# Sixteen of 22 feature tiles by seven products, and partial sums put into PSUM by ScalarE

## The chip, the cores and the metric

The kernel runs on one core of one Trainium2 chip. The metric is device time in microseconds of one execution: the median of 3 runs before the change is 2388.46 us (2387.38 to 2388.64). Engines are named as the profile names them: PE is TensorE (matmul), PEld its weight loads, DVE is VectorE, ACT is ScalarE, POOL is GpSimd, SP is SyncE, which issues the loads.

## The reference

Two layers; each is a feed-forward block, a mixing block of three kinds of attention, and a second feed-forward block, with a norm ahead of and behind each. The change touches the four feed-forward blocks alone. 512 tokens, model width 1024, feed-forward width 2816 = 22 tiles of 128 features.

```python
D_MODEL, SEQ, DEPTH = 1024, 512, 2
D_FF = ((8 * D_MODEL // 3 + 127) // 128) * 128        # 2816

def _swiglu(t, w_gate, w_up, w_down):
    return (jax.nn.silu(t @ w_gate) * (t @ w_up)) @ w_down

for l in range(DEPTH):
    f = _swiglu(_rmsnorm(h, ffn1_pre_g[l]), ffn1_w_gate[l], ffn1_w_up[l], ffn1_w_down[l])
    h = h + 0.5 * _rmsnorm(f, ffn1_post_g[l])
    ...                                               # mixing: three attentions, gates, output product
    f = _swiglu(_rmsnorm(h, ffn2_pre_g[l]), ffn2_w_gate[l], ffn2_w_up[l], ffn2_w_down[l])
    h = h + 0.5 * _rmsnorm(f, ffn2_post_g[l])
```

## The kernel before, in words

**Arithmetic.** Every factor is split into a high and a low part (`split`: ScalarE casts the high part, VectorE subtracts for the low part), and `mm3` makes one product of three matmuls of 128x512: high by high (L214), low by high (L215 or L216), high by low. The four feed-forward blocks are called a0, c0 (first layer) and a1, c1.

**Feature tiles in three ways.** Of the 22 feature tiles of a block, tiles 0 and 1 are "halved": they are made in two halves of the tokens, so that they can begin before the norm is done for all tokens (`halved`, L801 and L802). Plain pairs (14 and 15, 16 to 21) are made feature-major, with `gates` and `ups`, at full width. Twelve tiles (2 to 13) are made in three groups of four (`group`, `gate_up`): the input is cut into two halves of the tokens and of the width, the weights (two gate tiles and two up tiles side by side) likewise, and a 2x2 block product is made from seven block products in place of eight. `ORDER = (0, 2, 3, 4, 5, 1, 6)` is the order of the seven; `BlockUnit` makes their weights (one or two loads of 512 KB, up to two VectorE passes of 128x1024, a cast by ScalarE and a low part by VectorE), and `sums` with `whole`, `block_sum` and `parts_of` makes the sums of the input's blocks (L679, L685, L188, L189). The result of a group is token-major and is turned into feature-major by 16 transposes (`feature_major`, L761).

The seven products of a group write three pairs of PSUM banks: product 0 opens one that 3, 5 and 6 go on with; product 2 opens one that 4 goes on with; product 1 has its own. After a product, the banks are copied out by ScalarE or added to a tile `c..` in SBUF by VectorE (L744).

**Down.** The first 16 feature tiles go through `downs(0)` and `downs(1)`, again by seven block products (`product`, `first_factor`), the last six in `down` (plain), whose results VectorE adds to what lies in SBUF (`down_out`, L827; at the kernel's end `last_part`, L580). The seven products of `downs` are woven with the last plain pairs.

**What sets the order.** A queue `Q` holds jobs (weights to load, a generator that yields matmuls); loads are made ahead of their jobs as rings allow. Then a scheduler orders each engine's instructions within the dependences. PSUM has eight banks: four with the tag "mm" and four with the tag "z". Weight parts have rings of four (`wh`, `wl`).

Of the kernel before, what the change touches and what calls it, by code (L numbers as in the profile page):

```python
# [22 lines left out]
def kernel(  # L23
# [494 lines left out]
    class Sub:  # L518
# [57 lines left out]
        def last_part(self, t, hf, c, pt, i):  # L576

            f, h, st = self.fs[t], hT[t], self.sf[t]
            s, fc, w = tmp(f"fe{i}"), f[:, HF[hf]][:, c], slice(0, c.stop - c.start)
            nc.vector.tensor_tensor(s[:, w], fc, pt, ALU.add)  # L580
            self.squared(s[:, w], st, 2 * i, s[:, S // 2:])
            nc.vector.scalar_tensor_tensor(fc, s[:, w], RS * (0.5 if self.half else 1.0), self.gp[:, HF[hf]][:, c],
                                           ALU.mult, ALU.mult)
# [54 lines left out]
    TG = (2, 6, 10)  # L638

    HR = ("q", "q", "o", "o", "o", "tri", "tri", "rs")  # L640
    ORDER = (0, 2, 3, 4, 5, 1, 6)

    def ffn(l, src, wg, wu, wd, dst, name, spare, aside=None):
# [9 lines left out]
        def hidden(f, pg, pu):  # L653
            s = tmp(f"s{name}_{f}")
            nc.scalar.activation(s[:], pg[:], AF.Silu)
            if f < NC * FC:
                nc.vector.tensor_tensor(pair(f)[:, f % 2], pu[:], s[:], ALU.mult)
                return
            nc.vector.tensor_tensor(s[:], pu[:], s[:], ALU.mult)
            t = blk("q" if f >= 20 else "o", f"hid{name}_{f}")  # L660
# [61 lines left out]
        def gate_up(f, n, uns):  # L722
            if n in (0, 1, 2):
                st["gb", SUM[n]] = [pbank("mm", f"pt{name}_{f}_{n}_{e}") for e in range(2)]
            pts = st["gb", SUM[n]]
            opens, ends = n in (0, 1, 2), n in (1, 4, 6)
            for un in uns:
                for k in range(un.nk):
                    kk = un.k0 + k
                    for e in range(2):  # L730
                        mm3(pts[e][:], *input_block(n, kk, e), un.h[:, k], un.l[:, k], opens and kk == 0,
                            ends and kk == ND // 2 - 1, free=True)
                        yield 3 * S * PE_US
            i, j = TO[n]
            if n in (0, 2, 3, 6):
                st["c", i, j] = stile([P, 2, S], "f", f"c{name}_{f}_{i}{j}", F32)
            t = st["c", i, j]
            for e in range(2):
                if n == 6:
                    nc.scalar.activation(t[:, e], pts[e][:], AF.Silu)  # L740
                elif n in (0, 2, 3):
                    nc.scalar.copy(t[:, e], pts[e][:])
                else:
                    nc.vector.tensor_tensor(t[:, e], t[:, e], pts[e][:], ALU.add)  # L744
            if n == 1:
                nc.scalar.activation(t[:], t[:], AF.Silu)
            if n in (1, 6):
                u = st["c", i, 1]
                nc.vector.tensor_tensor(u[:], u[:], t[:], ALU.mult)
                st["hid", f, i] = u  # L750

        def feature_major(f):

            for i in range(2):
                u = st.pop(("hid", f, i))
                for b in range(2):
                    f2 = f + 2 * b
                    pt = pbank("z", f"th{name}_{f2}_{i}")
                    for m in range(2):
                        for e in range(2):  # L760
                            nc.tensor.transpose(pt[:, (2 * m + e) * P:(2 * m + e + 1) * P],  # L761
                                                u[:, e, (2 * b + m) * P:(2 * b + m + 1) * P], ident[:])
                    yield 0.45
                    out_ = pt[:].rearrange("p (m q) -> p m q", m=2)
                    nc.scalar.copy(pair(f2)[:, :, HALVES[i]], out_)

        def group(f):

            keep = Keep(lambda i, k0: stile([P, 2, S], "v", f"kt{name}_{f}_{i}_{k0}", F32)[:])
            for n in ORDER:  # L770
# [4 lines left out]
                yield uns, (lambda n=n, uns=uns: gate_up(f, n, uns))  # L775
            yield [], lambda: feature_major(f)
# [7 lines left out]
        def halved(f, ug, uu, half):  # L784
            if half == 0:
                st["p"] = [pbank("mm", f"p{x}{name}_{f + m}") for x in "gu" for m in range(2)]
            else:
                Q.hold, Q.pinned = False, True
                Q.load_ahead()
                Q.pinned = False  # L790
            c = HALVES[half]
# [29 lines left out]
        def down_out(t, hf, pt, last):  # L821
            f = dst.fs[t][:, HF[hf]]
            if not last:
                nc.vector.tensor_tensor(f, f, pt, ALU.add)
                return f
            s = tmp(f"f{name}_{t}")
            nc.vector.tensor_tensor(s[:], f, pt, ALU.add)  # L827
            return s[:]
# [28 lines left out]
        def product(ci, n, uns):  # L857
# [4 lines left out]
            if n in (0, 1, 2):  # L862
# [3 lines left out]
            opens, ends = n in (0, 1, 2), n in (1, 4, 6)  # L866
# [40 lines left out]
        def plain(f, *n):  # L907

            ug = wpair(wg[l], ND, f * P, f"g{name}_{f}")
            uu = wpair(wu[l], ND, f * P, f"u{name}_{f}")  # L910
            Q.add(ug, lambda: gates(f, ug))
            some(n[0])
            behind()
            Q.add(uu, lambda: ups(f, uu))
            some(n[1])

# [9 lines left out]
        ug, uu = wpair(wg[l], ND, 0, f"g{name}_0"), wpair(wu[l], ND, 0, f"u{name}_0")  # L926
# [3 lines left out]
        Q.add(ug + uu, lambda: halved(0, ug, uu, 0), src.ready((0, 1)))  # L930
        Q.add([], lambda: halved(0, ug, uu, 1), src.ready(range(NT)))
        Q.add([], lambda: iter(park() or ()))
        marks["first"] = len(Q.jobs)
        summed = sums()
        todo = iter([([], lambda: iter(next(summed) or ()))] * 3)
        plain(14, 1, 1)
# [3 lines left out]
        some(1)  # L940
        todo = turns(2)
        some(7)
        for g in (6, 10):
# [6 lines left out]
        todo = iter(())  # L950
        pairs = [(wpair(wg[l], ND, f * P, f"g{name}_{f}"), wpair(wu[l], ND, f * P, f"u{name}_{f}")) for f in (16, 18)]
        Q.add(pairs[0][0], lambda: gates(16, pairs[0][0]))
        behind()
        todo = downs(0)
# [8 lines left out]
        xg, xu = wpair(wg[l], ND, 20 * P, f"g{name}_20"), wpair(wu[l], ND, 20 * P, f"u{name}_20")  # L963
        Q.add(xg, lambda: gates(20, xg))
# [3 lines left out]
        Q.add(xu, lambda: ups(20, xu))  # L968
# [11 lines left out]
        down(wd[l, f0 * P:], NF - f0, hact, down_out, f"d{name}", dst, marks, reload)  # L980
        return marks

    def down(w, ktiles, act, emit, name, dst, marks, before=None):
# [7 lines left out]
        PAIRS = ((0, 1), (2, 3))  # L991

        def tiles(uns, hf, ts, done=None):
            pts = [pbank("mm", f"p{name}_{hf}_{t}") for t in ts]
            for un in uns:
                for k in range(un.nk):
                    kk = un.k0 + k
                    for t, pt in zip(ts, pts):
                        ah, al = act(kk, slice(t * P, (t + 1) * P))
                        mm3(pt[:], ah, al, un.h[:, k], un.l[:, k], kk == 0, kk == ktiles - 1)  # L1000
                        yield 3 * S * PE_US
                if done is not None:
                    done()
            last = len(ts) == 1
            for t, src in [(t, emit(t, hf, pt[:], last)) for t, pt in zip(ts, pts)]:
                dst.result(t, hf, src)

        def at_last(uns, hf, t):

            parts = [(c, pbank("mm", f"p{name}_{hf}_{t}_{i}")) for i, c in enumerate(HALVES)]  # L1010
            for i, (c, pt) in enumerate(parts):
                for un in uns:
                    for k in range(un.nk):
                        kk = un.k0 + k
                        ah, al = act(kk, slice(t * P, (t + 1) * P))
                        mm3(pt[:, c], ah, al, un.h[:, k, c], un.l[:, k, c], kk == 0, kk == ktiles - 1)
# [3 lines left out]
        def late(uns, hf, t):  # L1020
            if t == NT - 1 and dst.g_pre is None and hf == 0:
# [727 lines left out]
```

## Time and profile before

| | |
|---|---|
| median of 3 runs | 2388.46 us |
| span of the profiled execution | 2385.9 us |
| median less span | 2.6 us |
| granted clock | 1.000 |
| TensorE busy | 2374.6 us, 11720 instructions |
| TensorE weight loads | 2009.0 us |
| VectorE busy | 1834.2 us, 2525 instructions |
| ScalarE busy | 1317.5 us, 2136 instructions |

The profiled execution is told by its span, from the first to the last instruction; its own time outside the span isn't shown, and the median is 2.6 us above the span. Rows of the timeline give start, duration, engine, line, operation, out<-in and shape; what stands in brackets is idle time just before and what ended it. The groups of a view by line give a count and the least, middle and largest duration in ns.

### The profile page before, as it was taken

To read this page: it belongs to the slowest core of one execution; us is meant where nothing else is said; L and a number is where in the kernel's file an instruction comes from. 1 tells how busy PE (TensorE), PEld (TensorE's weight loads), DVE (VectorE), ACT (ScalarE), POOL (GpSimd) and SP (SyncE) were. 2 spreads that over 40 slices of the span, in tenths; PEclk is the share of its full clock that TensorE was granted. 3 is DMA by queue.
4 is the path that set the end of the run, shared out by engine and by line. 5 is a ranking of instruction groups with operands and counts; after the bars stand their busy time and mean duration, and the time that the engine had idled before them with its cause. 6 is when DMAs were issued, how large, how long until landed. Compare 5 with 4: busy or idle time off the path is not lost.

```text
span 2385.9 us, 30907 instructions
## 1 busy us (share of the span) xinstructions
PE 2374.6 (100%) x11720; PEld 2009.0 (84%) x11720; DVE 1834.2 (77%) x2525; ACT 1317.5 (55%) x2136; POOL 74.0 (3%) x130
## 2 busy tenths in 40 slices
PE   9999999999999999999999999999999999999998
PEld 8888888888888898888898888888888888988887
DVE  7786877678777687778787878776787766778686
ACT  5655555677655554554545554556675655455443
POOL 0000000001110000000000000000001100000000
PEclk9999999999999999999999999999999999999999
DMA  5554664222323445545544536532232244445453
GB/s 188 166 174 136 202 212 151 71 76 76 89 67 120 150 133 177 168 150 194 185 142 159 185 133 231 184 115 80 63 89 80 73 139 142 159 142 185 141 203 124
DMA packets 234265, 337.13 MB, mean 141 GB/s; under 512 B 10346, under 2 KB 133506, under 8 KB 233604
## 3 DMA queue, kind: packets, MB, share of 16 engines
q1 hardware_dynamic: 234016, 335.13, 43.2%
q8 instruction: 92, 1.51, 0.3%
q14 instruction: 57, 0.47, 0.1%
q0 software_dynamic: 96, 0.03, 0.0%
q10 hardware_dynamic: 4, 0.00, 0.0%
HBM read 320.44 MB, written 14.68 MB: 140 GB/s over the span
## 4 chain that ended last, share of the span: by engine, by line
PE 95%; DVE 2%; DMA 1%; ACT 1%; issue 0%; DVEq 0%; ACTq 0%
PE pg L216 4%; PE pg L214 4%; PE pg L215 4%; PE pta L214 3%; PE pta L216 3%; PE pta L215 3%; PE pdc L214 3%; PE pdc L215 3%; PE pdc L216 3%; PE ptc L215 3%; PE ptc L216 3%; PE ptc L214 3%; PE pda L215 3%; PE pda L216 3%; PE pda L214 3%; PE pb L214 2%
## 5 line engine op out<-in xcount | busy, mean ns | idle before, releaser
L214 PE MATMUL pg<-us_a,wh_wg 128*128 128x512 f32 x384 | 151.0, 393 | 0.0
L216 PE MATMUL pg<-us_a,wl_wg 128*128 128x512 f32 x384 | 149.7, 390 | 0.0
L215 PE MATMUL pg<-us_a,wh_wg 128*128 128x512 f32 x384 | 149.6, 390 | 0.0
L188 ACT CAST wh_tc<-ktc 128x1024 fp32r<-128x1024 f32 x60 | 62.6, 1052 | 83.3 <-DVE ktc L349 37.2
L188 ACT CAST wh_ta<-kta 128x1024 fp32r<-128x1024 f32 x60 | 62.6, 1052 | 80.9 <-DVE kta L349 34.5
L189 DVE TENSOR_TENSOR wl_tc<-ktc,wh_tc 128x1024 fp32r<-128x1024 f32 x60 | 72.8, 1222 | 25.1 <-ACT wh_tc L188 24.9
L189 DVE TENSOR_TENSOR wl_ta<-kta,wh_ta 128x1024 fp32r<-128x1024 f32 x60 | 72.8, 1222 | 24.2 <-ACT wh_ta L188 23.9
L215 PE MATMUL pda<-wl_da,aha 128*128 128x512 f32 x224 | 87.1, 389 | 0.0
L216 PE MATMUL pda<-wh_da,ala 128*128 128x512 f32 x224 | 87.1, 389 | 0.0
L214 PE MATMUL pda<-wh_da,aha 128*128 128x512 f32 x224 | 87.1, 389 | 0.0
L215 PE MATMUL pdc<-wl_dc,ahc 128*128 128x512 f32 x224 | 87.1, 389 | 0.0
L214 PE MATMUL pdc<-wh_dc,ahc 128*128 128x512 f32 x224 | 87.1, 389 | 0.0
L216 PE MATMUL pdc<-wh_dc,alc 128*128 128x512 f32 x224 | 87.1, 389 | 0.0
L216 PEld LDWEIGHTS pg<-us_a,wl_wg 128*128 128x128 f32 x384 | 72.1, 188 | 15.2
L215 PEld LDWEIGHTS pg<-us_a,wh_wg 128*128 128x128 f32 x384 | 72.2, 188 | 14.1
L214 PEld LDWEIGHTS pg<-us_a,wh_wg 128*128 128x128 f32 x384 | 72.1, 188 | 14.1
L192 DVE SCALAR_TENSOR_TENSOR wl_wg<-raw_wg,wh_wg 128x1024 fp32r<-128x1024 f32 x48 | 58.6, 1220 | 25.9 <-ACT wh_wg L191 25.3
L214 PE MATMUL pta<-wh_ta,aga 128*128 128x512 f32 x192 | 75.1, 391 | 0.0
L214 PE MATMUL ptc<-wh_tc,agc 128*128 128x512 f32 x192 | 75.1, 391 | 0.0
L215 PE MATMUL ptc<-wl_tc,agc 128*128 128x512 f32 x192 | 74.8, 390 | 0.2 <-DVE wl_tc L189 0.2
L216 PE MATMUL pta<-wh_ta,aga 128*128 128x512 f32 x192 | 74.7, 389 | 0.0
L216 PE MATMUL ptc<-wh_tc,agc 128*128 128x512 f32 x192 | 74.7, 389 | 0.0
(536 smaller groups left out, 7675.8 us busy)
## 6 DMA issues: line engine op xcount, KB each, us to landing
raw_da<-in_ffn_w_down_dram SPq DMA_DIRECT2D x58, 512.0 KB, 3.7
raw_dc<-in_ffn_w_down_dram SPq DMA_DIRECT2D x58, 512.0 KB, 3.3
raw_ta<-in_ffn_w_gate_dram SPq DMA_DIRECT2D x48, 512.0 KB, 3.7
raw_wg<-in_w_gate_dram SPq DMA_DIRECT2D x48, 512.0 KB, 3.6
raw_tc<-in_ffn_w_gate_dram SPq DMA_DIRECT2D x48, 512.0 KB, 3.7
kta<-in_ffn_w_up_dram SPq DMA_DIRECT2D x24, 512.0 KB, 4.9
raw_wo<-in_w_out_dram SPq DMA_DIRECT2D x24, 512.0 KB, 3.3
ktc<-in_ffn_w_up_dram SPq DMA_DIRECT2D x24, 512.0 KB, 4.9
```

The source lines that it names most:

```text
L188: both = [nc.scalar.copy(h_ap, src)]
L189: make = lambda: nc.vector.tensor_tensor(l_ap, src, h_ap.bitcast(F32), ALU.subtract)
L192: make = lambda: nc.vector.scalar_tensor_tensor(l_ap, src, scale, h_ap.bitcast(F32), ALU.mult, ALU.subtract)
L214: nc.tensor.matmul(pt, lh, rh, start=start, stop=False, skip_group_check=free)
L215: nc.tensor.matmul(pt, lh, rl, start=False, stop=False, skip_group_check=free)
L216: nc.tensor.matmul(pt, ll, rh, start=False, stop=stop, skip_group_check=free)
```

## The change

In each feed-forward block, 16 tiles (0 to 15, `TG = (0, 4, 8, 12)`) are now made by groups, two (16 and 17) are halved, and 18 to 21 are plain. The pair 14 and 15 that was plain beside the input's sums is gone: the first group follows the halved tiles directly, and the sums of the input's blocks are spread between its jobs (`add_sums`, and one step in `halved`). The first group has its own order, `FIRST = (0, 1, 2, 3, 4, 5, 6)`; the others keep `ORDER`. The last group is turned not in the "z" banks but in the "mm" banks, since the first products of `downs(0)` come before it.

Partial sums: where product 1 comes after product 4, ScalarE copies (`seeds`) what was summed in SBUF into two PSUM banks, and the matmuls of product 1 accumulate on it; VectorE's adds after product 1 go, and ScalarE's Silu or copy reads the banks. The same holds for `product` of the down stage, and for `down` with `carry=True`, where the banks are put a step ahead (`seed`, `AFTER`), so that `down_out` and `last_part` add no more.

The diff, cut to its core:

```diff
-    TG = (2, 6, 10)
-    HR = ("q", "q", "o", "o", "o", "tri", "tri", "rs")
+    TG = (0, 4, 8, 12)
+    EARLY = NC * FC
+    HR = ("o", "o", "o", "o", "o", "o", "tri", "tri")
     ORDER = (0, 2, 3, 4, 5, 1, 6)
+    FIRST = (0, 1, 2, 3, 4, 5, 6)
...
-        def gate_up(f, n, uns):
-            if n in (0, 1, 2):
+        def seeds(tag, name, parts):
+            banks = [pbank(tag, f"{name}_{e}") for e in range(len(parts))]
+            for pt, part in zip(banks, parts):
+                nc.scalar.copy(pt[:], part)
+            return banks
+
+        def gate_up(f, n, uns, last_of_top):
+            seeded = ("gb", 1) in st if n == 1 else False
+            if n in (0, 1, 2) and not seeded:
                 st["gb", SUM[n]] = [pbank("mm", f"pt{name}_{f}_{n}_{e}") for e in range(2)]
...
             for e in range(2):
-                if n == 6:
+                if n == 6 or seeded:
                     nc.scalar.activation(t[:, e], pts[e][:], AF.Silu)
                 elif n in (0, 2, 3):
                     nc.scalar.copy(t[:, e], pts[e][:])
                 else:
                     nc.vector.tensor_tensor(t[:, e], t[:, e], pts[e][:], ALU.add)
-            if n == 1:
+            if n == 1 and not seeded:
                 nc.scalar.activation(t[:], t[:], AF.Silu)
-            if n in (1, 6):
+            if n == 4 and last_of_top == 1:
+                st["gb", 1] = seeds("mm", f"pt{name}_{f}_1", [st["c", 0, 0][:, e] for e in range(2)])
+            if n == 6 or n == last_of_top:
...
-                    pt = pbank("z", f"th{name}_{f2}_{i}")
+                    pt = pbank("mm" if f == TG[-1] else "z", f"th{name}_{f2}_{i}")
...
         def group(f):
+            order = FIRST if f == TG[0] else ORDER
+            top = max((1, 4), key=order.index)
...
-        def down_out(t, hf, pt, last):
+        def down_out(t, hf, pt, seeded):
+            if seeded:
+                return pt
             f = dst.fs[t][:, HF[hf]]
...
+            nc.vector.tensor_tensor(f, f, pt, ALU.add)
+            return f
... (in product, the down stage)
-                if ci == 0 and n in (0, 2, 3, 6):
+                if n == 1 or ci == 0 and n in (0, 2, 3, 6):
                     nc.scalar.copy(f, pts[e][:])
                 else:
                     nc.vector.tensor_tensor(f, f, pts[e][:], ALU.add)
+            if n == 4:
+                st["b", 1] = seeds("z", f"pd{name}_{ci}_1", [dst.fs[e][:, HF[0]] for e in range(2)])
... (the order of the jobs)
-        plain(14, 1, 1)
+        add_sums()
+        todo = turns(TG[0])
+        some(1)
+        add_sums()
+        some(7)
...
-        Q.add(pairs[0][0], lambda: gates(16, pairs[0][0]))
-        behind()
         todo = downs(0)
-        Q.add(pairs[0][1], lambda: ups(16, pairs[0][1]))
+        some(2)
+        Q.add(pairs[0][0], lambda: gates(18, pairs[0][0]))
+        behind()
         some(3)
-        Q.add(pairs[1][0], lambda: gates(18, pairs[1][0]))
+        Q.add(pairs[0][1], lambda: ups(18, pairs[0][1]))
         some(7)
-        Q.add(pairs[1][1], lambda: ups(18, pairs[1][1]))
         todo = downs(1)
...
-        down(wd[l, f0 * P:], NF - f0, hact, down_out, f"d{name}", dst, marks, reload)
+        down(wd[l, f0 * P:], NF - f0, hact, down_out, f"d{name}", dst, marks, reload, carry=True)
...
+        def seed(hf, ts):
+            for t, b in AFTER.get((ts[0], hf), ()) if carry else ():
+                parts = HALVES if halves(b, t) else (FULL,)
+                banks[t, b] = [pbank("mm", f"p{name}_{b}_{t}_{i}") for i in range(len(parts))]
+                for pt, c in zip(banks[t, b], parts):
+                    nc.scalar.copy(pt[:, c], dst.fs[t][:, HF[b]][:, c])
```

Counted in the built program, whole kernel: 96 matmuls of 128x512 fewer and 64 transposes more on TensorE; on VectorE 64 operations of 128x1024 more and 55 of 128x512 fewer; on ScalarE 24 casts of 128x1024, 119 operations of 128x512 and 16 of 2x256 more; 24 loads of 512 KB more.

More of the change, by code (lines that the diff above doesn't have):

```diff
@@ L578, in last_part @@
             f, h, st = self.fs[t], hT[t], self.sf[t]
[L579 to L582, printed above, removed]
+            s, fc = tmp(f"fe{i}"), f[:, HF[hf]][:, c]
+            self.squared(pt, st, 2 * i, s[:, S // 2:])
+            nc.vector.scalar_tensor_tensor(fc, pt, RS * (0.5 if self.half else 1.0), self.gp[:, HF[hf]][:, c],
                                            ALU.mult, ALU.mult)
@@ L730, in gate_up @@
                     for e in range(2):
-                        mm3(pts[e][:], *input_block(n, kk, e), un.h[:, k], un.l[:, k], opens and kk == 0,
+                        mm3(pts[e][:], *input_block(n, kk, e), un.h[:, k], un.l[:, k], opens and kk == 0 and not seeded,
                             ends and kk == ND // 2 - 1, free=True)
@@ L790, in halved @@
                 Q.pinned = False
+                next(summed)
             c = HALVES[half]
@@ L865, in product @@
             h, l = st["a", ci, n]
[L866 removed]
+            opens, ends = n in (0, 2), n in (1, 4, 6)
             for un in uns:
@@ L939, in ffn @@
             Q.add([], lambda: iter(mem_stats() or ()))
[L940 to L943, printed above, removed]
+        for g in TG[1:]:
             todo = turns(g)
@@ L962, in ffn @@
         norm = aside() if aside is not None else None
-        xg, xu = wpair(wg[l], ND, 20 * P, f"g{name}_20"), wpair(wu[l], ND, 20 * P, f"u{name}_20")
-        Q.add(xg, lambda: gates(20, xg))
+        Q.add(pairs[1][0], lambda: gates(20, pairs[1][0]))
         some(4)
@@ L999, in tiles @@
                         ah, al = act(kk, slice(t * P, (t + 1) * P))
-                        mm3(pt[:], ah, al, un.h[:, k], un.l[:, k], kk == 0, kk == ktiles - 1)
+                        mm3(pt[:], ah, al, un.h[:, k], un.l[:, k], kk == 0 and not seeded, kk == ktiles - 1, seeded)
                         yield 3 * S * PE_US
+                    if kk == 1:
+                        seed(hf, ts)
                 if done is not None:
                     done()
-            last = len(ts) == 1
-            for t, src in [(t, emit(t, hf, pt[:], last)) for t, pt in zip(ts, pts)]:
+            for t, src in [(t, emit(t, hf, pt[:], seeded)) for t, pt in zip(ts, pts)]:
                 dst.result(t, hf, src)
         def at_last(uns, hf, t):
-            parts = [(c, pbank("mm", f"p{name}_{hf}_{t}_{i}")) for i, c in enumerate(HALVES)]
+            parts = [(c, pt) for c, pt in zip(HALVES, banks.pop((t, hf)))]
             for i, (c, pt) in enumerate(parts):
@@ L1020, in late @@
         def late(uns, hf, t):
-            if t == NT - 1 and dst.g_pre is None and hf == 0:
+            if halves(hf, t):
                 yield from at_last(uns, hf, t)
```

56 lines of the change are left out of this document (22 added, 34 removed).

## The prediction, made before the changed kernel had run

> **What bounds the kernel now.** I read the head of the page first, then its chain of waits, then the view of what TensorE waits for.
>
> ```profile
> span 2385.9 us, 30907 instructions
> PE 2374.6 (100%) x11720; PEld 2009.0 (84%) x11720; DVE 1834.2 (77%) x2525; ACT 1317.5 (55%) x2136; POOL 74.0 (3%) x130
> PE 95%; DVE 2%; DMA 1%; ACT 1%; issue 0%; DVEq 0%; ACTq 0%
> PE pts L1186 <- ACT ts L1217: 1.5, 2, 0.7
> PE warm L1619 <- DVE warm L1703: 1.3, 1, 1.3
> ...
> PE ptc L215 <- DVE wl_tc L189: 0.2, 1, 0.2
> ```
>
> The reader is to see that TensorE (PE) is 95% of the chain and that its waits (microseconds in all, times, longest) are small: the largest is 1.5 us. Nothing else sets the time. So a matmul that goes saves its full pitch, and every wait that comes new costs its full length. One row matters later: product 2 or 3 of a group waited once, 0.2 us, for a low part from VectorE (DVE), so VectorE runs just ahead in the group stages. The median is 2388.46, the profiled span 2385.9; 2.6 us lie outside the span, and I leave them as they are. The sums are made in the span and added to the median.
>
> The pitch of matmuls and transposes comes from the timeline of TensorE, in the second feed-forward block (c0):
>
> ```profile
> 999.66 0.39 PE L215 MATMUL ptc<-wl_tc,agc 128*128 128x512 f32 x1
> 999.89 0.39 PE L216 MATMUL ptc<-wh_tc,agc 128*128 128x512 f32 x1
> ...
> 1009.41 0.39 PE L216 MATMUL ptc<-wh_tc,agc 128*128 128x512 f32 x1
> 951.26 1.91 PE L761 MATMUL thc<-ident,cc 128*128 128x128 f32 x16
> 952.92 0.48 PE L214 MATMUL ptc<-wh_tc,agc 128*128 128x512 f32 x1
> ```
>
> From 999.66 to 1009.41 there are 43 steps: 9.75 / 43 = 0.2267 us per 128x512 matmul (the 0.39 shown overlaps the next). Sixteen transposes take 952.92 - 951.26 = 1.66, or 0.104 each. A product of a group has 8 k-steps-by-halves of three matmuls, 24 in all: 5.44 us.
>
> **Part 1, work taken from TensorE.** Counted in the built program, the change takes away 96 matmuls of 128x512 (two tiles more through the seven products, in each of four blocks: 24 per block) and adds 64 transposes: -96 x 0.2267 = -21.8, +64 x 0.104 = +6.7, together **-15.1 us**. At the end of the kernel the last part loses its add:
>
> ```profile
> 2379.01 0.41 DVE L580 TENSOR_TENSOR fe<-fc,pdc 128x256 f32<-128x256 f32 x1
> ```
>
> It stands between the last matmul and the norm, so **-0.4**. The other 54 or so adds that VectorE loses (0.68 each, row in part 3) are not on the path, since TensorE does not wait for them now.
>
> **Part 2, the first group of each block.** Only this group goes 0, 1, 2, 3, 4, 5, 6 and is not seeded at product 1. Products 0, 1 and 2 each open two banks of the four "mm" ones. Product 0's pair lives on (3, 5 and 6 accumulate there), so product 2 needs product 1's pair, which VectorE frees with the two adds into `c00`. In the built program of the change, those adds stand here in VectorE's queue of c0 (item numbers are places in the queue):
>
> ```
>  990 low of agc_2           1003,1004 block sums (k-tiles of product 3)
>  991,992 hidden 16,17       1005,1006 lows of agc_4, agc_5
>  993 r00                    1007 low of wl_0_3_0
>  994,995 lows of hid 16,17  1008 low of wl_0_3_2
>  996 low of agc_3           1009 c00 += pt_1_0   (128x512)
>  997..1002 six of 128x1024  1010 c00 += pt_1_1   (128x512)
> TensorE: products 0, 1; nine matmuls of product 3 (need wl_0_3_0); product 2 (waits for VectorE)
> ```
>
> Where VectorE stands at that time is told by its timeline before, since up to `agc_2` both programs give it the same nine operations from `rc` on:
>
> ```profile
> 880.38 0.28 PE L802 MATMUL puc<-us_b,wl_uc 128*128 128x256 f32 x1
> 880.50 0.40 PE L214 MATMUL pgc<-us_b,wh_gc 128*128 128x512 f32 x1
> 870.07 1.21 DVE L679 TENSOR_TENSOR rc<-us_b 128x1024 f32<-128x1024 f32 x1
> 871.20 2.35 DVE L189 TENSOR_TENSOR wl_gc<-raw_gc,wh_gc 128x1024 fp32r<-128x1024 f32 x2
> 873.47 2.35 DVE L679 TENSOR_TENSOR rc<-us_b 128x1024 f32<-128x1024 f32 x2
> 880.92 1.22 DVE L189 TENSOR_TENSOR agc<-rc,agc 128x1024 fp32r<-128x1024 f32 x1 [0.20 <-ACT agc L188]
> 882.07 1.28 DVE L657 TENSOR_TENSOR hrc<-puc,sc 128x512 f32<-128x512 f32 x2
> 883.27 3.73 DVE L685 TENSOR_TENSOR rc<-rc,rc 128x1024 f32<-128x1024 f32 x3
> ```
>
> The halved pair ends and whole-width products begin at 880.50. A 128x1024 operation holds VectorE 1.14 us ((873.47 - 871.20) / 2), a 128x512 one 0.60 ((883.27 - 882.07) / 2). Items 991 and 992 are done at 883.27; then one of 1.14 (993), two of 0.60, eleven of 1.14 (996 to 1006): item 1007 starts at 883.27 + 1.14 + 1.20 + 12.54 = 898.15, ends at 899.37; 1008 starts at 899.29, 1009 at 900.43 and, 0.68 long, ends at 901.11. Products 0 and 1 end at 880.50 + 10.88 = 891.38. Between 891.38 and 901.11 TensorE has only those nine matmuls to do (2.04): it loses 9.73 - 2.04 = **7.7 us**, and I take as much for a1 and c1, where `agc_2` or `aga_2` comes 0.61 and 0.88 us after the first whole-width matmul, against 0.42 in c0:
>
> ```profile
> 1223.12 0.40 PE L214 MATMUL pga<-us_c,wh_ga 128*128 128x512 f32 x1
> 1223.73 1.23 DVE L189 TENSOR_TENSOR aga<-ra,aga 128x1024 fp32r<-128x1024 f32 x1 [0.20 <-ACT aga L188]
> 2062.91 0.40 PE L214 MATMUL pgc<-us_b,wh_gc 128*128 128x512 f32 x1
> 2063.79 1.23 DVE L189 TENSOR_TENSOR agc<-rc,agc 128x1024 fp32r<-128x1024 f32 x1 [0.20 <-ACT agc L188]
> ```
>
> What queues behind is everything: matmuls are kept in order, and all of the block follows product 2.
>
> The first block (a0) has a fuller queue and weights that are just arriving:
>
> ```profile
> 37.92 0.40 PE L214 MATMUL pga<-us_x,wh_ga 128*128 128x512 f32 x1
> 39.28 1.28 DVE L657 TENSOR_TENSOR hra<-pua,sa 128x512 f32<-128x512 f32 x2
> 40.84 1.23 DVE L189 TENSOR_TENSOR wl_ua<-raw_ua,wh_ua 128x1024 fp32r<-128x1024 f32 x1 [0.28 <-ACT wh_ua L188]
> 52.72 1.22 DVE L337 TENSOR_TENSOR kta<-kta,raw_ta 128x1024 f32<-128x1024 f32 x1 [0.36 <-DMA raw_ta<-in_ffn_w_gate_dram]
> 56.11 1.23 DVE L337 TENSOR_TENSOR kta<-kta,raw_ta 128x1024 f32<-128x1024 f32 x1 [0.95 <-DMA raw_ta<-in_ffn_w_gate_dram]
> ```
>
> Products 0 and 1 and the two small transposes end at 37.92 + 10.88 + 0.2 = 49.0. After the hidden pair (done at 40.48 by the pitch) VectorE has a low, two of 0.60, and fourteen more of 1.14 ahead of the first add: 40.48 + 15 x 1.14 + 1.20 = 58.78, and the add ends at 59.46. Lost: 59.46 - 49.0 - 2.04 = 8.4 with no wait on VectorE's side; the rows show it waiting 0.28, 0.36 and 0.95 (1.6 in all) for casts and transfers here, and half of that makes **9.2 us**. The four holes: 3 x 7.7 + 9.2 = **32.3 us**. Bounds: 28, if part of the low parts moves ahead of their place by an earlier start of the block; 40, if VectorE waits 2 us more per block for transfers.
>
> [...]
>
> [...] The "z" banks are idle in this stage; with product 2 in them TensorE would wait only for `wl_0_3_0` after product 2, 899.37 - (891.38 + 5.44) = 2.6 us a block in place of 7.7. [...]
>
> **Part 3, the turn of the last group, now in "mm" banks.** The gates of tiles 18 and 19 hold two of the four, so the third and fourth bank of transposes wait for ScalarE's copies of the first and second. In ScalarE's queue the first copy stands behind a weight cast that waits for a buffer, which the last gates matmul (start G) frees.
>
> ```profile
> 115.63 0.39 PE L216 MATMUL pta<-wh_ta,aga 128*128 128x512 f32 x1
> 116.06 0.59 ACT L742 COPY ca<-pta 128x512 f32<-128x512 f32 x1 [0.94 <-PE pta L216]
> 878.41 1.05 ACT L188 CAST wh_uc<-raw_uc 128x1024 fp32r<-128x1024 f32 x1 [0.38 <-DMA raw_uc<-in_ffn_w_up_dram]
> 879.36 0.59 ACT L655 ACTIVATE sc<-pgc 128x512 f32<-128x512 f32 x1
> 879.85 1.04 ACT L188 CAST agc<-rc 128x1024 fp32r<-128x1024 f32 x1
> L744 DVE TENSOR_TENSOR cc<-cc,ptc x36: 676/680/687, 923.8 to 2198.7; 128x512 f32<-128x512 f32 x36
> ```
>
> ScalarE follows a matmul's start by 0.43; a cast holds it 0.95 (879.36 - 878.41), a 128x512 operation 0.49. Cast at G + 0.43, first copy at G + 1.38, ends at 1.97; another copy of 0.49 lies between, so the second starts at 2.36 and ends at 2.95. TensorE, in place of 16 transposes running on from G + 0.23 to 1.89, does the last four from 2.95 to 3.37: **1.5 us, four times 6.0**. Bounds 0 (the buffer comes free earlier) and 8.
>
> **Part 4, what I price at nothing or nearly.** Seeds: after product 4 VectorE's two adds (1.2) and ScalarE's two copies must be done before product 1. The trace has no copy from SBUF into PSUM; the nearest rows are the copies out (0.59, above). 0.45 + 1.28 + 2 x 0.59 is 2.9 us against product 5's 5.44, which hides them; if ScalarE came 2.5 us late, each group would pay the rest. ScalarE gets some 90 us more, on 55%. VectorE gains 64 of 128x1024 and loses 55 of 128x512: 64 x 1.14 - 55 x 0.60 = +40 us, on 77%. The stage it is fullest in:
>
> ```profile
> 38.00:60.00 22.00, 22.00 (x99) 17.94 (x97) 19.09 (x19) 9.47 (x11) 0.00 (x0) 1.00 0.81 265
> 98.00:138.00 40.00, 40.00 (x186) 33.39 (x185) 33.73 (x32) 21.80 (x28) 0.00 (x0) 1.00 0.57 187
> ```
>
> (Columns: length, then PE, PEld, DVE, ACT busy.) In a group it is busy 33.73 of 40, so a fourth group can be fed as the three are. SP issues 24 more loads of 512 KB, at a DMA share of 0.57 there. I take one more wait of 0.2, as in the first fence, for each block: **0.8**, up to 6.
>
> **Sum:** -15.1 - 0.4 + 32.3 + 6.0 + 0.8 = +23.6; 2388.46 + 23.6 = **2412 us**.
>
> **Rivals.**
> *The hole is covered (faster, chance 0.08).* VectorE would have to reach the adds before 891.4, i.e. have nine of the operations from 993 to 1008 out of the way or behind. Against: the built order; for: it starts the block's sums as soon as the norm gives them, and a shorter stage before could shift it 1 to 2 us. Then -15.1 - 0.4 + 6.8: 2380; with the turn hidden too, 2373. It decides below 2.7 us per hole ((15.5 - 4.8) / 4, 4.8 us being the 0.2% that a measurement of this kernel can tell).
> *Holes only (0.22).* The turn's copies run at once: 2412 - 6 = 2406.
> *VectorE is the bound throughout (0.10).* With +40 us of work its lead is used up, and each of sixteen groups pays 0.2 (the row) to 0.5, 3 to 8 us, and the holes are 40, not 32.3: 2423 to 2428.
> *No net change (0.04).* Holes of half the size, 16, with the turn hidden: 2389.
> My forecast itself has 0.56.
>
> **Range and chances.** Low 2400 takes holes of 28 with a turn of 0 (2388.46 - 15.5 + 28 = 2401); high 2425 takes 38 with 6 and 2 more elsewhere, short of 40 with 8 and 6. Faster 0.08, within 0.2% 0.04, slower 0.88.
>
> **What would show it.** In the profile after: four waits of TensorE, of 5 to 10 us each in sum, for `wl_t…_3_0` and for the banks of product 1, at about 49, 891, and at the same place in a1 and c1; VectorE without a gap there; four stops of about 1.5 us at the transposes of the last group, released by ScalarE; 96 matmuls fewer. It is wrong if TensorE's idle time stays below 15 us, or if stalls stand at product 1 of seeded groups.

## The result: 1.63% slower, and the profile after

The changed kernel takes 2427.4 us (median of 4 runs, 2426.5 to 2428.4) against 2388.3 of the kernel before: a ratio of 1.0163, 95% interval 1.0149 to 1.0178. The forecast was 2412 with a range up to 2425, so the measured time lies above the range. The direction came out, and so did the place of the stops in the first groups; the size fell short by 15 us.

The head of the page after:

```profile
span 2426.6 us, 31086 instructions
PE 2380.1 (98%) x11688; PEld 2003.4 (83%) x11688; DVE 1872.7 (77%) x2532; ACT 1402.5 (58%) x2291; POOL 74.1 (3%) x130
```

There are 32 instructions fewer on TensorE (96 matmuls less, 64 transposes more), yet it is busy 5.5 us longer: some matmuls got slower. What TensorE waits for (us in all, times, longest):

```profile
PE pta L214 <- ACT wh_ta L188: 11.7, 2, 6.7
PE ptc L214 <- ACT wh_tc L188: 9.8, 2, 4.9
PE ptc L215 <- DVE wl_tc L189: 3.5, 3, 1.5
PE pta L215 <- DVE wl_ta L189: 3.0, 2, 1.5
PE pta L214 <- ACT ca L747: 1.9, 2, 1.0
...
PE pga L216 <- DVE wl_ga L189: 1.0, 2, 0.5
PE pgc L216 <- DVE wl_gc L189: 0.9, 2, 0.5
PE thc L768 <- ACT hrc L772: 0.8, 2, 0.5
PE tha L768 <- ACT hra L772: 0.3, 1, 0.3
```

The first four rows hold the stops of the four first groups: two in each block, one for the high part of product 3's weights, one for its low part. The profile puts the longer one down to ScalarE, but ScalarE itself had waited 3.43 us there for a sum of VectorE:

```profile
907.50 1.99 ACT L188 CAST agc<-rc 128x1024 fp32r<-128x1024 f32 x2 [3.43 <-DVE rc L683]
909.39 1.99 ACT L188 CAST wh_tc<-ktc 128x1024 fp32r<-128x1024 f32 x2
```

VectorE at that place, in c0:

```profile
903.98 2.35 DVE L189 TENSOR_TENSOR wl_tc<-ktc,wh_tc 128x1024 fp32r<-128x1024 f32 x2
906.25 1.22 DVE L683 TENSOR_TENSOR rc<-rc,rc 128x1024 f32<-128x1024 f32 x1
907.38 2.35 DVE L340 TENSOR_TENSOR ktc<-ktc,ktc 128x1024 f32<-128x1024 f32 x2
909.65 2.35 DVE L189 TENSOR_TENSOR agc<-rc,agc 128x1024 fp32r<-128x1024 f32 x2
911.92 2.35 DVE L189 TENSOR_TENSOR wl_tc<-ktc,wh_tc 128x1024 fp32r<-128x1024 f32 x2
914.19 1.28 DVE L749 TENSOR_TENSOR cc<-cc,ptc 128x512 f32<-128x512 f32 x2
```

It has no gap, and the adds that free the banks (L749) come last, as the queue said. TensorE (the number in brackets is the wait just before; a start-to-start distance is longer by a matmul):

```profile
905.20 0.39 PE L216 MATMUL ptc<-wh_tc,us_b 128*128 128x512 f32 x1
910.49 1.22 PE L214 MATMUL ptc<-wh_tc,agc 128*128 128x512 f32 x2 [4.90 <-ACT wh_tc L188]
913.20 0.80 PE L215 MATMUL ptc<-wl_tc,agc 128*128 128x512 f32 x1 [1.49 <-DVE wl_tc L189]
913.79 0.63 PE L216 MATMUL ptc<-wh_tc,agc 128*128 128x512 f32 x1
914.22 0.63 PE L215 MATMUL ptc<-wl_tc,agc 128*128 128x512 f32 x1
...
916.35 0.63 PE L214 MATMUL ptc<-wh_tc,agc 128*128 128x512 f32 x1
...
918.48 0.43 PE L216 MATMUL ptc<-wh_tc,agc 128*128 128x512 f32 x1
918.75 0.39 PE L214 MATMUL ptc<-wh_tc,agc 128*128 128x512 f32 x1
```

The new thing is the pitch: from 913.79 to 914.22 a matmul takes 0.43 us, not 0.2267, and so until 918.48. The tenth matmul behind product 1, at 916.35, is product 2's first by the built order; by then the first add had ended (914.19 + 0.68 = 914.87), so no wait for banks shows in the profile. From 905.20 to 918.75 there are 16 matmuls: 13.55 - 16 x 0.2267 = 9.9 us lost, against 7.7 forecast. The same sum over a0, a1 and c1 gives 10.9, 10.0 and 9.7; all four 40.5, against 32.3. The granted clock (before the last two numbers of a row):

```profile
905.40:915.10 9.70, 3.31 (x8) 2.03 (x8) 9.70 (x10) 3.88 (x4) 0.00 (x0) 0.65 0.10 37
915.10:918.50 3.40, 3.40 (x10) 2.63 (x9) 0.37 (x1) 1.06 (x1) 0.00 (x0) 0.50 0.00 0
```

In the second stretch TensorE is busy throughout at a clock of 0.50, while VectorE worked 0.37 us of 3.40, ScalarE 1.06, and no transfer ran. Contention is an unlikely cause there; the fourth experiment tests it.

The rest, by block: from its first halved matmul to the first matmul behind it a block took 343.2, 342.6, 340.2 and 340.3 us before and takes 356.4, 352.5, 349.0 and 348.5, where the work taken away (24 matmuls less 16 transposes) should have made it 3.8 shorter. So TensorE loses 17.0, 13.7, 12.6 and 12.0 us, 55.3 in all, of which the holes are 40.5. 4.1 lie in a0's second group, 3.6 at the gates of tiles 20 and 21, 2.4 at the turn of the last group (its transposes), 2.3 at the start of second groups, 1.4 at the start of the first, the rest in single stops under 1 us (each the time beyond the pitches in its stretch). The blocks together grew by 40.1, the span by 40.7.

### The profile page after: what moved, and what is told of

Read it like the earlier page. It is cut to its first block, busy times and chain, and to the rows that moved or that the text cites. A ratio compares the mean times of both kernels' runs of the same rounds, so it can differ in the third digit from the quotient of the medians.

```text
span 2426.6 us, 31086 instructions
## 1 busy us (share of the span) xinstructions
PE 2380.1 (98%) x11688; PEld 2003.4 (83%) x11688; DVE 1872.7 (77%) x2532; ACT 1402.5 (58%) x2291; POOL 74.1 (3%) x130
## 4 chain that ended last, share of the span: by engine, by line
PE 81%; DVE 8%; DMA 4%; ACT 3%; issue 2%; POOL 0%; DVEq 0%; ACTq 0%; POOLq 0%
PE pg L216 3%; PE pg L214 3%; PE pg L215 3%; PE ptc L215 3%; PE ptc L216 3%; PE pta L215 3%; PE ptc L214 3%; PE pta L216 3%; PE pta L214 3%; PE pdc L214 2%; PE pdc L215 2%; PE pdc L216 2%; PE pda L215 2%; PE pda L214 2%; PE pda L216 2%
## 5 line engine op out<-in xcount | busy, mean ns | idle before, releaser
L188 ACT CAST wh_ta<-kta 128x1024 fp32r<-128x1024 f32 x80 | 83.3, 1053 | 92.2 <-DVE kta L337 26.2
L188 ACT CAST wh_tc<-ktc 128x1024 fp32r<-128x1024 f32 x80 | 83.2, 1051 | 88.1 <-DVE ktc L337 24.4
L189 DVE TENSOR_TENSOR wl_tc<-ktc,wh_tc 128x1024 fp32r<-128x1024 f32 x80 | 96.8, 1222 | 35.9 <-ACT wh_tc L188 35.5
L189 DVE TENSOR_TENSOR wl_ta<-kta,wh_ta 128x1024 fp32r<-128x1024 f32 x80 | 96.9, 1222 | 33.6 <-ACT wh_ta L188 33.3
L214 PE MATMUL pta<-wh_ta,aga 128*128 128x512 f32 x256 | 102.9, 404 | 13.6 <-ACT wh_ta L188 11.7
L214 PE MATMUL ptc<-wh_tc,agc 128*128 128x512 f32 x256 | 102.4, 401 | 9.8 <-ACT wh_tc L188 9.8
L215 PE MATMUL ptc<-wl_tc,agc 128*128 128x512 f32 x256 | 102.2, 399 | 3.5 <-DVE wl_tc L189 3.5
L215 PE MATMUL pta<-wl_ta,aga 128*128 128x512 f32 x256 | 102.6, 401 | 3.0 <-DVE wl_ta L189 3.0
L216 PE MATMUL pta<-wh_ta,aga 128*128 128x512 f32 x256 | 101.9, 398 | 0.0
L216 PE MATMUL ptc<-wh_tc,agc 128*128 128x512 f32 x256 | 101.6, 397 | 0.0
```

Source lines behind the costliest of these rows:

```text
L188: both = [nc.scalar.copy(h_ap, src)]
L189: make = lambda: nc.vector.tensor_tensor(l_ap, src, h_ap.bitcast(F32), ALU.subtract)
L214: nc.tensor.matmul(pt, lh, rh, start=start, stop=False, skip_group_check=free)
L215: nc.tensor.matmul(pt, lh, rl, start=False, stop=False, skip_group_check=free)
L216: nc.tensor.matmul(pt, ll, rh, start=False, stop=stop, skip_group_check=free)
```

## The experiments

Theories: **A**, VectorE is late in the first group, and product 2 stands behind product 3's first matmuls because the banks it needs are freed at the end of VectorE's queue; **B**, VectorE cannot keep up with the first group whatever the banks; **C**, the slow matmuls behind a stop are the clock; others where they come. Ratios are to the kernel before on the same chip.

**Other banks for product 1.**

```diff
-                st["gb", SUM[n]] = [pbank("mm", f"pt{name}_{f}_{n}_{e}") for e in range(2)]
+                st["gb", SUM[n]] = [pbank("z" if n == 1 else "mm", f"pt{name}_{f}_{n}_{e}") for e in range(2)]
```

> Product 1 of the first group writes two z banks in place of mm banks; nothing else. Theory A (product 2 stands still for banks that VectorE frees late in its queue): product 2 starts right behind product 1, what is left is the wait for the low parts of products 2 and 3, some 2.2 us in c0, a1, c1 and some 5 us in a0, in place of 9.9 and 10.9 in the changed kernel; 2427 - 3 x 7.6 - 5.9 = 2398 us (2394 to 2404). Rival B (VectorE cannot keep up with the first group at all): the stop only moves on to products 3 to 5, 2418 or more.

Measured 2399.8 us (1.0051, 1.0036 to 1.0066): A. TensorE in c0:

```profile
904.43 0.61 PE L214 MATMUL ptc<-wh_tc,agc 128*128 128x512 f32 x2
906.78 0.50 PE L215 MATMUL ptc<-wl_tc,agc 128*128 128x512 f32 x1 [1.73 <-DVE wl_tc L189]
907.12 0.39 PE L216 MATMUL ptc<-wh_tc,agc 128*128 128x512 f32 x1
907.35 0.40 PE L215 MATMUL ptc<-wl_tc,agc 128*128 128x512 f32 x1
```

Product 2 runs without a stop, and the one wait left there is 1.73 us for product 3's low part, which the prediction gave as 2.6. One line of code takes back 27.6 us. Behind this wait the pitch is full again from the second matmul on (907.35 - 907.12 = 0.23).

**The sums one job later.**

```diff
         todo = turns(TG[0])
-        some(1)
-        add_sums()
-        some(7)
+        some(2)
+        add_sums()
+        some(6)
```

> The third step of the input's sums (one whole, one block sum, two low parts) is queued behind product 1, not product 0; banks as in the changed kernel. Theory A: the adds that free the banks move ahead of the low part of product 3 in VectorE's queue, so product 2 starts some 5.5 us earlier in each block: 2405 us (2400 to 2412). Rival B: VectorE's work is the same, only put off, and the stop comes back at product 4: 2420 or more.

Measured 2408.4 (1.0084, 1.0069 to 1.0099): A, within its range. The order in VectorE's queue sets the stop: in c0 one wait of 3.10 us is left of the two of 4.90 and 1.49. Behind this wait the granted clock is 0.50 (903.80 to 906.50); behind one just as long in c1, in the same execution, it is 1.00 (2092.50 to 2095.20).

**Both.**

> Both edits: z banks for product 1 of the first group, and the third step of the sums behind product 1. Theory A: no stop of more than 1 us is left in the first group of c0, a1 and c1, 2 to 3 us in a0: 2391 us (2387 to 2397). Rival B: 2405 or more, since the VectorE work comes due at product 4.

Measured 2399.1 (1.0052, 1.0033 to 1.0071): a miss of 8 us; it is no better than the z banks alone. The waits tell where the gain went:

```profile
PE pta L214 <- ACT ca L747: 4.0, 3, 2.0
PE ptc L214 <- ACT wh_tc L188: 1.9, 2, 1.0
PE pta L214 <- ACT wh_ta L188: 1.9, 2, 1.0
PE thc L768 <- DVE cc L756: 1.9, 2, 1.0
```

The waits for `wl_tc` are gone, and new ones stand at the group's end: the transposes wait for VectorE's product of gate and up (L756), and copies and casts are late. So B holds in part: work put off inside the first group comes due before it ends.

**Twenty idle matmuls in the hole.** They keep TensorE at work; their result is read by nobody.

```diff
+            if n == 1 and not seeded:
+                st["filler"] = pbank("z", f"filler{name}")
+            if n == 2 and "filler" in st:
+                fill = st.pop("filler")
+                for r in range(20):
+                    nc.tensor.matmul(fill[:], input_block(1, 3, 0)[0], act(0)[0], start=r == 0, stop=r == 19)
```

> Twenty matmuls of 128x512 whose result nobody reads (a z bank, operands that lie ready) stand between product 1 and what follows in the first group: 4.5 us of TensorE work inside a stop of 5 to 7 us. Theory C (the 427 ns pitch behind a stop is the granted clock, which falls because TensorE stood idle): the matmuls behind it run at 227 ns, product 2 starts when VectorE frees its banks, some 1.5 us earlier, and runs at full pace, 1 us more: 4 x 2.5 less, 2417 us (2413 to 2421). Rival D (the pitch is contention with VectorE's and ScalarE's work at that time): 427 ns stay, 2427 (2424 to 2431).

Measured 2418.3 (1.0127, 1.0112 to 1.0142): C. With 80 matmuls more the kernel is 9.1 us faster.

```profile
901.90:911.60 9.70, 7.67 (x33) 5.73 (x32) 9.70 (x10) 3.90 (x4) 0.00 (x0) 1.00 0.08 29
```

Product 1 of c0 ends 3.4 us earlier in this run, so this is the stretch that had 0.65 before: the clock is 1.00, with VectorE as busy as there (9.70 of 9.70 us). That leaves idle time of TensorE, not contention, as the cause of the slow matmuls. The slow pitch in the changed kernel is (916.35 - 914.22) / 5 = 0.426 us. How long it lasts differs from place to place: the clock was full again after 5.3 us of work in c0 (913.20 to 918.48), 3.1 in a0 (58.78 to 61.87), and 2.7 with the sums one job later (903.80 to 906.53). Waits shorter than the 4.90 of c0 lowered the clock in places too, 3.10 us in that last run and 2.17 us in a later one (the plain pair put back in front). The prediction had no term for slow matmuls behind a stop.

**The change without its seeds.** VectorE's adds as before, 16 tiles by groups.

```diff
-            if n == 4 and last_of_top == 1:
+            if False:
...
-            if n in (0, 2):
+            if n in (0, 1, 2):
                 st["b", SUM[n]] = [pbank("z", f"pd{name}_{ci}_{n}_{e}") for e in range(2)]
...
-        down(wd[l, f0 * P:], NF - f0, hact, down_out, f"d{name}", dst, marks, reload, carry=True)
+        down(wd[l, f0 * P:], NF - f0, hact, down_out, f"d{name}", dst, marks, reload)
```

> The changed kernel with the other half undone: no partial sum is put into PSUM, VectorE adds as before in the groups, the down stage and the last products; 16 tiles by groups as changed. Theory A (the loss is in the first groups and behind their stops): the first-group stops stay as they are, 2428 us (2424 to 2432). Rival E (ScalarE's copies into PSUM make the other stops, at the second group of a0 and at the turn of the last group): 2420 or less.

Measured 2432.3 (1.0178, 1.0163 to 1.0194), 0.3 us above A's range and far from E. The interval with seeds is 1.0149 to 1.0178, so the two overlap: that the seeds gain anything in the changed kernel is not shown, and neither is the 5 us that a later expectation takes from here.

**The seeds alone**, in the kernel before: the same edits the other way round.

> The kernel before with the seeds alone: product 1 and the last products accumulate on partial sums that ScalarE puts into PSUM; 12 tiles by groups as before, the order of the jobs as before. Theory A: TensorE does not wait for the adds that go, so only the add in the last chain is saved: 2388 us (2385 to 2390). Rival E (the copies cost stops of their own): 2394 or more.

Measured 2387.5 (0.9994, 0.9986 to 1.0003): no difference that can be told. Adds that TensorE does not wait for are worth nothing measurable, and the 0.4 us for the last add is too small to see.

**The memory's statistics moved** to the end of a0, on top of the z banks.

```diff
-            Q.add([], lambda: iter(mem_stats() or ()))
...
         Q.add(pairs[1][1], lambda: ups(20, pairs[1][1]))
+        if name == "a0":
+            Q.add([], lambda: iter(mem_stats() or ()))
```

> The z banks for product 1 of the first group, and the statistics of the memory (two passes of 128x1024 and four table loads of 1.28 us on ScalarE) moved from behind the first group of a0 to behind its last ups. Theory: the stop of 5.0 us in a0's second group, where ScalarE copies banks out late, was made by these: 2395 us (2393 to 2397). Rival: ScalarE is late there because of seeds and casts: 2399.

Measured 2404.3 (1.0065, 1.0052 to 1.0079): a miss. It was to be faster than the z banks alone and isn't (1.0036 to 1.0066 there; the intervals overlap, so it isn't shown to be slower either). The stop it aimed at is real: in the changed kernel ScalarE, in a0's second group, loads tables between bank copies,

```profile
104.80 1.28 ACT L1078 ACT_TABLE_LOAD   x1
106.10 0.20 ACT L1078 ACTIVATE mem_rstd<-mem_rstd 128x1 f32<-128x1 f32 x1
106.21 0.57 ACT L747 COPY ca<-pta 128x512 f32<-128x512 f32 x1
106.79 1.28 ACT L1079 ACT_TABLE_LOAD   x1
```

and TensorE's wait for these copies, 2.9 us with z banks alone, is gone once the statistics are moved. But the normed memory is wanted straight after the new place, and TensorE waits there instead:

```profile
PE mt L1107 <- DVE mraw L1101: 4.5, 2, 2.8
```

**Three sums on GpSimd**, on top of that.

```diff
-            nc.vector.tensor_tensor(r, *(st["r", x // 10, x % 10][:] for x in (a, b)), op)
+            eng = nc.gpsimd if n in (4, 5) else nc.vector
+            eng.tensor_tensor(r, *(st["r", x // 10, x % 10][:] for x in (a, b)), op)
```

(and `whole(0, 1)` likewise)

> As the one with z banks and moved statistics; besides, three of the input's sums (whole 0 1, block sums 4 and 5; 3 x 1.14 us of VectorE per block) run on GpSimd. Theory A (VectorE's work comes due too early in the first groups): the stops left there, some 4 us in a0 and 3 us in c0, a1 and c1, fall by half or more: 2389 us (2385 to 2393). Rival F (GpSimd is much slower than VectorE, and low parts of the sums wait for it): 2397 or more.

Measured 2418.7 (1.0126, 1.0112 to 1.0139): rival F, and the rows show a reason beside its own. F's own is there: the add takes GpSimd 2.4 to 2.7 us, VectorE 1.14. GpSimd and VectorE at the same time, in c0:

```profile
898.92 2.69 POOL L678 TENSOR_TENSOR rc<-us_b 128x1024 f32<-128x1024 f32 x1 [5.85 <-DVE rc L685]
901.70 2.72 POOL L685 TENSOR_TENSOR rc<-rc,rc 128x1024 f32<-128x1024 f32 x1
```

```profile
899.28 2.89 DVE L189 TENSOR_TENSOR hidc<-sc,hidc 128x512 fp32r<-128x512 f32 x1
902.09 3.41 DVE L189 TENSOR_TENSOR agc<-rc,agc 128x1024 fp32r<-128x1024 f32 x1
```

While GpSimd adds, an operation of VectorE that takes 0.68 or 1.22 elsewhere takes 2.89 or 3.41, and ends 0.56 or 1.08 us after GpSimd's add, about its own length. So each of these two adds cost VectorE 2.2 us, 4.4 together, where all three moved were to save it 3.4. How much of the loss is due to each reason stays open.

**The plain pair put back in front.** The pair 18 and 19 stands behind the halved tiles and no longer among the products of `downs(0)`, with the sums behind its gates and ups, as 14 and 15 did; all groups in `ORDER`.

```diff
-    FIRST = (0, 1, 2, 3, 4, 5, 6)
+    FIRST = ORDER
...
+        Q.add(pairs[0][0], lambda: gates(18, pairs[0][0]))
         add_sums()
-        todo = turns(TG[0])
-        some(1)
+        Q.add(pairs[0][1], lambda: ups(18, pairs[0][1]))
         add_sums()
-        some(7)
...
+        add_sums()
+        todo = turns(TG[0])
+        some(7)
```

> The changed kernel, but the plain pair 18 and 19 is made directly behind the halved tiles, with one step of the input's sums behind the gates, one behind the ups and one ahead of the first group, as the kernel before did with 14 and 15; all four groups in the old order and seeded. Theory A (VectorE's twelve passes for the sums had their cover in the 21.8 us of the plain pair, and the change took it away): no stop in the first groups, 2388.5 - 15.2 and up to 3.5 at the gates of 20 and 2 at the turn: 2376 us (2373 to 2382), faster than both. Rival G (a fourth group and the seeds cannot be fed wherever the pair stands): 2390 or more.

Measured 2392.8 (1.0021, 1.0012 to 1.0030): the holes are gone as A said, but it is 17 us more than expected. The next run takes back 11 of them at the gates of 20, which the expectation had at up to 3.5:

```profile
PE pga L214 <- ACT wh_ga L188: 3.2, 2, 1.6
PE pgc L214 <- ACT wh_gc L188: 2.7, 2, 2.2
PE pta L214 <- ACT ca L747: 1.9, 1, 1.9
PE pda L216 <- DVE ala L189: 1.9, 2, 1.0
```

```profile
1115.09 1.04 ACT L188 CAST wh_dc<-btc 128x1024 fp32r<-128x1024 f32 x1 [2.95 <-DVE btc L340]
1116.04 1.99 ACT L188 CAST wh_gc<-raw_gc 128x1024 fp32r<-128x1024 f32 x2
```

```profile
1104.00:1122.00 18.00, 15.83 (x63) 12.04 (x62) 17.11 (x21) 8.24 (x10) 0.00 (x0) 0.91 0.55 192
```

Now the down stages have lost a plain pair. Around the gates of 20, VectorE is busy 17.11 of 18 us; ScalarE's cast for the gates stands behind one that waits 2.95 us for VectorE; TensorE waits 2.17 us for it, and the clock falls to 0.50 (1118.10 to 1121.00). This run changes two things about the first group, the pair ahead of it and its order, in which product 2 comes ahead of product 1 and does not need its banks; it does not part them. The z banks, which free product 2 without the pair, left 10.0 us of waits for low parts in the four blocks, most of them in the first groups, which speaks for the pair; a run with the old order alone is missing.

**The gates of 20 one product earlier.**

```diff
         todo = downs(1)
-        some(3)
+        some(2)
...
         Q.add(pairs[1][0], lambda: gates(20, pairs[1][0]))
-        some(4)
+        some(5)
```

> As the one with the plain pair in front; besides, the gates of 20 and 21 stand before product 3 of the second down stage, not behind it, so that their low parts do not queue behind two block sums and two adds on VectorE. Theory: the stop of 0.6 to 0.8 us at the gates of 20 in each block goes: 3 us less than the one with the plain pair in front, 2373 us (2370 to 2379). Rival: it moves to product 3: no difference.

Measured 2381.7 (0.9977, 0.9968 to 0.9986): faster than both kernels, and by 11 us than the last one. The gain was mis-sized (3 expected): the expectation took the stop of 0.6 to 0.8 us a block from the changed kernel, and with the pair in front it was longer (2.17 us and a slow clock in c0). The same stretch:

```profile
1104.00:1122.00 18.00, 18.00 (x81) 14.93 (x80) 17.60 (x22) 8.99 (x11) 0.00 (x0) 1.00 0.45 157
```

VectorE is as full as before; TensorE no longer waits there.

**One table for the statistics.**

```diff
+        tc.keep_in_program_order(nc.scalar.preload_act_table_set("natural_log_exp_and_others"))
         for t in range(MT):
```

> As the one with the plain pair and the gates of 20 in front; besides, the statistics of the memory in a0 load one activation table that holds both their functions, not one for each. Theory: the stop of 2.5 us in a0's first group, where ScalarE copies a bank out late, goes or halves: 2379.5 us (2378 to 2382), against 2381.7 without. Rival: the stop is made by the passes themselves: 2381.7 stays.

Measured 2380.9 (0.9972, 0.9963 to 0.9982): not to be told from the last one. Among its waits is a new row:

```profile
PE ptc L215 <- DVE wl_tc L189: 1.5, 1, 1.5
```

The stop for `ca` in a0 is gone as the theory had it, but one of 1.5 us for `wl_tc` has come in c0, where nothing was edited. Why it came there stays open.

**The same without seeds**, edited as above.

> As the one with one table, without any seed: VectorE adds the partial sums as in the kernel before. 16 tiles by groups is then the only part of the change left. Theory: in the changed kernel the seeds were worth 5 us because VectorE was late there; with the plain pair in front VectorE has a lead in the groups, but the down stages are without a plain pair to cover them: 2379.5 + 1 to 5, 2382 us (2379 to 2386). Rival (VectorE's adds decide still): 2387 or more.

Measured 2386.9 (0.9997, 0.9988 to 1.0005): 6.0 us slower than with seeds, with intervals that do not meet (0.9963 to 0.9982 with). TensorE's waits for operands that VectorE makes come to 8.9 us without seeds and 6.0 with. Sixteen tiles by groups alone are worth nothing measurable here, the seeds alone were worth nothing measurable in the kernel before, and both together, with the pair in front, the gates moved and one table, are worth 0.28%.

## Why the prediction was right or wrong

**What bounds the kernel, and part 1.** Right. The profile after has the 32 instructions fewer that the counts give, 15.1 us at the pitches of the trace, and the blocks' growth of 40.1 us is in the span almost one to one (40.7). One reading is wrong and harmless: four tiles more go through the seven products, from 12 to 16, not two; the 24 matmuls per block belong to four.

**What failed.** Against a forecast of 23.6 us the median grew by 39.1 and the span by 40.7. Two terms were too small and one too large:

| term of the sum | forecast | measured |
|---|---|---|
| first groups (part 2) | 32.3 | 40.5 |
| turn of the last group (part 3) | 6.0 | 2.4 |
| everything else (part 4) | 0.8 | 12.4 |

**Part 2, the first group.** Place, order and queue were right: VectorE's adds began 20.8 us after the first whole-width matmul in c0 (914.19 against 893.4), 19.9 forecast. That they keep their place in the queue was taken as given there; in c0 VectorE ran items 990 to 1010 in the built order (894.76 to 914.19), and TensorE started no later matmul in the stop (905.20 to 910.49). As the experiments showed, other banks removed the long stop, and a later sum shortened it. The step that failed is the price of the nine matmuls and of those behind them: "nine matmuls of product 3 (2.04)" were taken at 0.2267 us, and they ran at 0.427. That is why product 2 began at 916.35, not at 914.87, the end of its first add, and six matmuls more were slow. The filler, which kept the clock up, gave back 9.1 us, more than the 8.2 by which the holes passed the forecast. The trace before had no such stop from which to price it.

**The idle "z" banks.** The prediction had a wait of 2.6 us a block in place of 7.7 with product 2 in them, 5.1 x 4 = 20.4 us; z banks for product 1 gave 27.6. The 20 did not hold the slow matmuls, which went with the long stops.

**Part 3, the turn.** Mis-sized, 2.4 for 6.0. The step took both gate banks of 18 and 19 as held. ScalarE's Silu of tile 18 stands ahead of the casts and frees one:

```profile
1083.27 0.59 ACT L656 ACTIVATE sc<-pgc 128x512 f32<-128x512 f32 x1
...
1084.78 1.99 ACT L188 CAST wh_dc<-btc 128x1024 fp32r<-128x1024 f32 x2
1086.68 0.58 ACT L772 COPY hrc<-thc 128x512 f32<-128x512 f32 x1
```

So the third bank need not wait: from 1085.30 TensorE does twelve transposes, three banks' worth, before it stops. The waits of all four turns are 1.1 us (the last two rows of the waits after).

**Part 4.** This is the larger failure. Seeds were as priced: TensorE waits for none, and the copies into PSUM took 0.58 us. But the 0.8 us for everything else was too small by 11.6 us, and the 12.4 measured are twice its own upper bound of 6. The step that failed is to take one row of the kernel before, a wait of 0.2 us, for stages whose order had changed. I had followed the first group and the turn through the queues, but not the statistics of the memory in a0's second group (4.1 us, two waits and the slow matmuls behind them), nor the gates of 20 and 21 (3.6). The experiments remove both waits, but no run gives either's price in the changed kernel, and what makes the rest of the 12.4 stays open.

**The range.** Its top does not follow from its terms: 38, 6 and 2 us more give 2388.46 - 15.5 + 46 = 2419, not 2425, and the outer bounds beside them, 40, 8 and 6, give 2427. The measured 2427.4 lies there by offsetting errors, since the turn took far less than 8 and the rest more than 6.

**The rivals.** The one on VectorE as the bound gave 2423 to 2428, where the time fell, but by luck: it had a wait in each of sixteen groups, and in c0 behind the first group TensorE is busy 39.91 of 40 us (932 to 972). VectorE is late in the first group, where the third experiment showed that its work comes due whatever the banks, and at the gates of 20 and 21. The holes were neither covered nor half covered.

## What to carry to other kernels

Ask of a stage that is taken away what it was covering: the plain pair was 21.8 us of TensorE work with little for VectorE in it, and the input's sums lived off it; put back in front, with the gates moved, the change gained 0.23%. Give the stages that you have not followed through the queues a price of their own too: here they cost 12.4 us, and 0.8 was forecast. Price a new stop of TensorE not by its length alone, but with the matmuls behind it: in the first groups here the clock was at half behind every wait of 4.12 to 6.75 us (behind 4.90 us a matmul took 0.427 us in place of 0.227), and behind some shorter ones; giving the engine idle work in the stop was 9.1 us cheaper here. Two halves of a change that are each worth nothing measurable can be worth something together, here where the one takes adds off the engine that the other fills.

## What the runs showed of the hardware

After a wait of 4.90 us (up to 910.49 in c0 of the changed kernel) matmuls of 128x512 went at 427 ns, and after a second wait of 1.49 us they did so until 5.3 us of steady work had passed; the clock in the profile was 0.50. The same pitch came after waits of 3.10 us (up to 903.80, with the sums one job later), of 2.17 us (up to 1117.14, with the plain pair in front), and after two of 0.89 and 1.02 us within 4 us (a0's second group, from 105.55 to 108.82). Waits of 1.73 us (up to 906.78, other banks), 1.96 us (up to 909.47, with the filler) and 2.28 us (up to 73.32, with the gates one product earlier) left the clock full (0.23 us a matmul behind the first two). So the length alone does not decide between 2 and 3 us: 2.17 halved the clock and 2.28 did not, and of two waits of 3.10 us in one execution one halved it (c0) and one did not (c1). All waits of 4 us and more in these first groups (4.12 to 6.75) halved it. With twenty idle matmuls in the gap of c0 it stayed at 1.00 (901.90 to 911.60). A GpSimd add of 128x1024 took 2.4 to 2.7 us in c0 (1.14 to 1.22 on VectorE), and two subtractions of VectorE that overlapped with one took 2.89 and 3.41 us in place of 0.68 and 1.22. A copy of 128x512 by ScalarE from SBUF into PSUM took 0.57 to 0.64 us (median 0.58) in the changed kernel, about as long as one out of PSUM (0.57 to 0.64, median 0.58 to 0.59).
